# Recurrence gates of a two-layer hybrid encoder: products block by block, with inputs and gate values laid out anew by way of DRAM

## The chip, the cores and the metric

The kernel runs on one core of one Trainium2 chip. The metric is the device time of one execution in microseconds (us); lower is better. Engines are named as the profile names them: PE multiplies matrices and writes PSUM, ACT (scalar), DVE (vector) and POOL compute on SBUF and PSUM, SP issues the DMAs from its queue. All of them run their own instructions strictly in the order of the program and wait for each other by semaphores.

## What is computed

The reference runs two layers over 256 tokens of 1024 channels. Each layer normalises its input, projects it with one wide matrix, and feeds three mixers: A (gated spatial product), B (latent attention) and C (a gated linear recurrence). Each mixer's output is gated and projected, the three are merged, projected once more, normalised and added. The change is in mixer C, whose two gates are products with 16 separate blocks of 80 x 80 weights:

```python
xb = xc.reshape(B, S, LRU_BLOCKS, LRU_BW)                # 16 blocks of 80 channels
r = jax.nn.sigmoid(jnp.einsum('bshi,hij->bshj', xb, w_a).reshape(B, S, C) + b_a)
i = jax.nn.sigmoid(jnp.einsum('bshi,hij->bshj', xb, w_x).reshape(B, S, C) + b_x)
log_a = -LRU_C * r * softplus(-lam)
a = exp(log_a)
bterm = sqrt(max(1 - exp(2 * log_a), 0)) * (i * xc)
h = scan over time of  h = a * h + bterm
```

All inputs are float32. Every weight and activation is split into a high part that the PE takes at its fast rate and a low rest, and a product is the sum of three: high x high, high x low, low x high.

## The kernel before

Channels lie on the 128 partitions and tokens on the free dimension, so most products are matmuls of a 128 x 128 piece of weights with 256 tokens. Weights come in *chunks* of up to 128 x 2048 floats, 1 MB each. `load` fills one of three `raw` buffers by a DMA on SP's queue. `split` has ACT copy it to `whi` (L268) and DVE subtract to get `wlo` (L269), into one of three pairs. A step that uses up a chunk calls `done` (by way of `fin`), which frees the pair, splits the next chunk and issues a load for the chunk after that. Table `LATE` says whether a step does this ahead of or behind its own work on ACT and DVE.

The steps of a layer are run in the order that the table `ORDER` spells out. One step is mostly one chunk: 48 matmuls into one PSUM buffer of 128 x 512. These buffers are taken in turn from two rings: `bank` hands out `mm0` to `mm4`, `aux` three more. A step that takes a buffer must wait until ACT or DVE has read what the buffer held five takes earlier.

The names that matter: `u` and `za` are products of mixer A (`gate_a` takes the buffer of `u`, another for z, then ACT makes a sigmoid at L847, DVE four products at L848 to L857, and `split_act` the high and low part of `ya`, ACT first, at L452). `ga`, `gb`, `gc` are merge gates (a sigmoid on ACT, L875). `pa`, `pb`, `pc` are the projections, whose result DVE multiplies into `acc` (L897). `zb` and `zc` are the gates of mixers B and C (sigmoid on ACT at L973, DVE at L974). For mixer C there are `split` (high and low part of the input, once for each half of 640 channels), `stack` (copies that line up pieces of it), `la` and `lx` (the two gates, one step for each half, written `la` 0, `la` 1 and so on), and `r1`, `r2`, `r3` (the recurrence: in `r1` ACT loads a table and takes five exponentials, L942, and five tanh, L944; DVE multiplies, L940).

The 80-wide blocks don't fit into 128 partitions evenly. So `lru_gate` works on five tiles of 128 channels in a half. Blocks that cross a tile's border need products with pieces of two tiles. That makes 4 matmuls for an even tile and 6 for an odd one, 24 for each gate and half. It takes two buffers of the `bank` ring and one of `aux`, and ACT writes the sigmoid into the slot that `r1` reads (L932). The weights of one gate and half are loaded as 16 small pieces into a buffer that POOL has cleared (L205, L210).

Of the kernel before, what the change touches and what calls it, by code (L numbers as in the profile page):

```python
# [34 lines left out]
R_Q, R_KV, R_LG, R_LB, R_CW, R_CB, R_BA, R_BX, R_LAM, R_N = 0, 3, 5, 13, 21, 61, 71, 81, 91, 101  # L35
# [5 lines left out]

COL_EVEN, COL_ODD, COL_STACK, LRU_N = 0, GT * P, (GT + 2) * P, (GT + 5) * P


STACKS = ((0, ((1, 0, 32),)), (4, ((3, 96, 32),)), (2, ((1, 96, 32), (3, 0, 16))))
SH = 32
# [8 lines left out]
    ("attend", 1), ("xc", 4), ("conv", 3), ("v", 1), ("conv", 4), ("uq", 3), ("attend", 2), ("split", 1),  # L55
    ("v", 2), ("v", 3), ("attend", 3), ("split", 0), ("norm", 0), ("u", 0), ("stack", 0), ("attend", 4),
# [10 lines left out]


SE = {
# [25 lines left out]
def tile_trunk(ctx: ExitStack, tc, I, out):  # L95
# [72 lines left out]
    for l in range(L):  # L168
        for j in range(4):
            c0, n = ((C_CQ, QR), (C_CQ + QR, KVR + HR))[j // 2]  # L170
            kind = "slot" if l and j == 3 else None
            add((l, "c", j), Chunk(4, n, proj("w_in", l, j % 2 * 4 * P, 4, c0, n), kind=kind))
        for key, j in ORDER:
            if key in COLS:
                c = Chunk(KT, CW, win(l, COLS[key] + j * CW))
            elif key == "uq":
                c = Chunk(3, 384, proj("mla_w_uq", l, 0, 3, j * 384, 384), kind="heads")
            elif key == "ukv":
                c = Chunk(2, 1024, proj("mla_w_ukv", l, 0, 2, j * 1024, 1024))
# [14 lines left out]
    def load(c, parts=1, mid=None):  # L194
# [10 lines left out]
        G.memset(c.raw[:, :n], 0.0)  # L205

        def piece(row, col, r0, c0, nr, ncol):

            b = r0 // BW
            nc.sync.dma_start(  # L210
                c.raw[row : row + nr, col : col + ncol],
                I[name][l, g * 8 + b, r0 - b * BW : r0 - b * BW + nr, c0 - b * BW : c0 - b * BW + ncol],
            )

        for b in range(8):
            for k in range(GT):
                r0, r1 = max(b * BW, k * P), min(b * BW + BW, k * P + P)
                if r0 < r1 and k % 2 == 0:
                    piece(r0 - k * P, COL_EVEN + b * BW, r0, b * BW, r1 - r0, BW)
                elif r0 < r1:  # L220
                    c0, c1 = max(b * BW, k * P), min(b * BW + BW, k * P + P)
                    piece(r0 - k * P, COL_ODD + k // 2 * P + c0 - k * P, r0, c0, r1 - r0, c1 - c0)
        for n_, (m, runs) in enumerate(STACKS):
            for k, r, nr in runs:
                for b in range(8):
                    r0, r1 = max(b * BW, k * P + r), min(b * BW + BW, k * P + r + nr)
                    c0, c1 = max(b * BW, m * P), min(b * BW + BW, m * P + P)
                    if r0 < r1 and c0 < c1:
                        piece(r0 - k * P - r, COL_STACK + n_ * P + c0 - m * P, r0, c0, r1 - r0, c1 - c0)

    def split(c, parts=1, mid=None):
# [27 lines left out]
        if c.lru:  # L259
            act(hi[:, :n], c.raw[:, :n], AF.Copy)  # L260
            st = slice(COL_STACK, n)
            act(hi[SH : 2 * SH, st], c.raw[:SH, st], AF.Copy)
            V.tensor_tensor(lo[:, :COL_STACK], c.raw[:, :COL_STACK], f(hi[:, :COL_STACK]), ALU.subtract)
            V.tensor_tensor(hi[2 * SH : 3 * SH, st], c.raw[:SH, st], f(hi[:SH, st]), ALU.subtract)
            return
# [190 lines left out]
    with tc.manual_schedule():  # L456
# [74 lines left out]
        for l in range(L):  # L531
# [168 lines left out]

            def conv_stack(g):

                _, xh, xl = cv[g]
                xs, two = slot("xs", (GT, S), F32R), xm
                for src, dst in ((xh, xs[:, 3:5]), (xl, two)):
                    copy(SE.get("wide", "V"), dst[:64], f(src[:64, 2:5:2]))
                    copy(SE.get("wide2", "A"), dst[64:], f(src[64:, 0:3:2]))
                for n, (_, runs) in enumerate(STACKS):
                    for p, src in enumerate((xh, xl, xh)):
                        at = p * SH  # L710
                        for k, r, nr in runs:
                            copy(SE.get(("thin", n, p), "V"), xs[at : at + nr, n], f(src[r : r + nr, k]))
                cv[g] += (xs, two)
# [193 lines left out]
            def lru_gate(key, row):  # L907
                def step(g):
                    _, xh, xl, xs, two = cv[g]
# [3 lines left out]
                    for m0 in range(0, GT, 2):  # L913
                        ms = range(m0, min(m0 + 2, GT))
                        ps = bank() if len(ms) == 2 else aux()
                        for m in ms:
                            pm = ps[:, (m - m0) * S : (m - m0 + 1) * S]
                            e = slice(COL_EVEN + m * P, COL_EVEN + m * P + P)
                            if m % 2:
                                d = slice(COL_ODD + m // 2 * P, COL_ODD + m // 2 * P + P)  # L920
                                mm3(pm, wh[:, d], wl[:, d], xh[:, m], xl[:, m], True, False)
                                mm3(pm, wh[:, e], wl[:, e], xs[:, 3 + m // 2], two[:, m // 2], False, True)
                            else:
                                n = (0, 4, 2).index(m)
                                d = slice(COL_STACK + n * P, COL_STACK + n * P + P)
                                mm3(pm, wh[:, e], wl[:, e], xh[:, m], xl[:, m], True, False)
                                mm(pm, wh[: 3 * SH, d], xs[: 3 * SH, n], start=False, stop=True)
                        if ms[-1] == GT - 1:
                            fin(c, key, 0)
                        for m in ms:  # L930
                            b = row + g * GT + m
                            act(o[:, m], ps[:, (m - m0) * S : (m - m0 + 1) * S], AF.Sigmoid, bias=pt[:, b : b + 1])  # L932
# [57 lines left out]
            def rows(_):  # L990
# [8 lines left out]
                "la": lru_gate("la", R_BA), "lx": lru_gate("lx", R_BX), "r1": recur1, "r2": recur2, "r3": recur3,  # L999
# [113 lines left out]
```

## Time and profile before

| | |
|---|---|
| median of 3 runs | 798.22 us (797.47 to 798.29) |
| the profiled execution | 798.34 us, of which the span in the trace is 796.6 us |
| instructions | 15355, of them 6445 matmuls |
| busy: PE | 788.1 us, 99% of the span |
| busy: DVE, ACT, POOL | 548.9, 469.3, 70.5 us |
| moved by DMA | 137.87 MB, 173 GB/s on average |

The profile's page gives busy times by engine and the groups of instructions by line. The timeline lists single instructions of an engine: start, duration, what it is, and in brackets how long the engine stood idle before it and for whom. The windows give busy time, the clock that the PE was granted (1.00 is full speed) and the DMAs' rate in a stretch.

### The profile page before, as it was taken

What the parts mean: (1) busy time and instruction counts of PE and PEld (TensorE: products, weight loads), DVE (VectorE), ACT (ScalarE), POOL (GpSimd) and SP (SyncE); (2) the same over time, 40 slices, a digit from 0 to 9 for tenths busy, and PEclk for the clock granted to TensorE, in tenths of its full rate; (3) what the DMA queues carried; (4) which work ended last, traced back from release to release, by engine and by line L of the source; (5) the groups of instructions that cost most, each with busy time, mean ns of one, the idle gap of its engine ahead of it and who ended that gap; (6) DMA issues with size and microseconds to landing.
All of it is one profiled execution on the core that took longest, in us unless ns stands there. A gap on an engine that the chain in (4) does not pass through costs nothing.

```text
span 796.6 us, 15355 instructions
## 1 busy us (share of the span) xinstructions
PE 788.1 (99%) x6445; PEld 780.2 (98%) x6445; DVE 548.9 (69%) x712; ACT 469.3 (59%) x689; POOL 70.5 (9%) x110
## 2 busy tenths in 40 slices
PE   9999999999999999999999999999999999999996
PEld 8999999999999999999999999999999999999996
DVE  5587788666876787555666868776578578775562
ACT  5785767339855736343567776654595584544441
POOL 1100503003000000000010032031210000000000
PEclk9999999999999999999999999999999999999998
DMA  7845454344666565666357626541575656564531
GB/s 229 290 152 182 153 161 155 112 122 137 201 213 211 159 215 169 199 212 216 109 171 239 208 94 211 159 128 51 166 219 167 221 162 202 185 214 150 193 132 54
DMA packets 134205, 137.87 MB, mean 173 GB/s; under 512 B 11046, under 2 KB 130808, under 8 KB 134136
## 3 DMA queue, kind: packets, MB, share of 16 engines
q1 hardware_dynamic: 134120, 136.90, 54.3%
q8 instruction: 50, 0.82, 0.4%
q14 instruction: 19, 0.16, 0.1%
q10 hardware_dynamic: 16, 0.00, 0.0%
HBM read 135.83 MB, written 1.05 MB: 172 GB/s over the span
## 4 chain that ended last, share of the span: by engine, by line
PE 94%; DMA 2%; issue 1%; DVE 1%; ACT 1%; SPq 0%; POOL 0%; POOLq 0%; DVEq 0%; ACTq 0%
PE mm L308 25%; PE mm L307 25%; PE mm L309 25%; PE mm L431 2%; PE mm L433 2%; PE mm L432 2%; DMA raw<-in_w_in_dram 1%; PE aux L843 1%; PE mm L730 1%; PE aux L770 1%; PE mm L731 1%; DMA X<-in_x_dram 1%; PE mm L549 1%; PE aux L1021 1%; PE mm L1020 1%
## 5 line engine op out<-in xcount | busy, mean ns | idle before, releaser
L269 DVE TENSOR_TENSOR wlo<-raw,whi 128x2048 fp32r<-128x2048 f32 (+5 forms) x123 | 264.6, 2156 | 115.9 <-ACT whi L268 115.5
L307 PE MATMUL mm<-hT,whi 128*128 128x256 f32 x1088 | 307.1, 282 | 0.0
L309 PE MATMUL mm<-hT,wlo 128*128 128x256 f32 x1088 | 305.8, 281 | 0.3 <-DVE wlo L269 0.3
L308 PE MATMUL mm<-hT,whi 128*128 128x256 f32 x1088 | 305.6, 281 | 0.0
L268 ACT ACTIVATE whi<-raw 128x2048 fp32r<-128x2048 f32 (+5 forms) x123 | 221.0, 1802 | 66.6 <-PE mm L308 26.8
L309 PEld LDWEIGHTS mm<-hT,wlo 128*128 128x128 f32 x1088 | 205.0, 188 | 0.5 <-DVE wlo L269 0.5
L307 PEld LDWEIGHTS mm<-hT,whi 128*128 128x128 f32 x1088 | 205.0, 188 | 0.0
L308 PEld LDWEIGHTS mm<-hT,whi 128*128 128x128 f32 x1088 | 205.0, 188 | 0.0
L973 ACT ACTIVATE t<-mm 128x512 f32<-128x512 f32 x18 | 10.8, 598 | 52.2 <-PE mm L309 52.2
L397 POOL TENSOR_TENSOR rstd<-rstd,mhalf 128x1 f32<-128x1 f32 x8 | 4.4, 551 | 391.1 <-DVE rstd L396 391.1
L308 PE MATMUL mm<-yc,whi 128*128 128x256 f32 x128 | 36.0, 282 | 0.0
L308 PE MATMUL mm<-ya,whi 128*128 128x256 f32 x128 | 36.0, 282 | 0.0
L307 PE MATMUL mm<-ya,whi 128*128 128x256 f32 x128 | 36.0, 281 | 0.0
L307 PE MATMUL mm<-yc,whi 128*128 128x256 f32 x128 | 36.0, 281 | 0.0
L431 PE MATMUL mm<-whi,hT 128*128 128x256 f32 x128 | 36.0, 281 | 0.0
L308 PE MATMUL mm<-yb,whi 128*128 128x256 f32 x128 | 35.9, 281 | 0.0
L309 PE MATMUL mm<-ya,wlo 128*128 128x256 f32 x128 | 35.9, 280 | 0.0
L309 PE MATMUL mm<-yc,wlo 128*128 128x256 f32 x128 | 35.9, 280 | 0.0
L309 PE MATMUL mm<-yb,wlo 128*128 128x256 f32 x128 | 35.8, 280 | 0.0
L307 PE MATMUL mm<-yb,whi 128*128 128x256 f32 x128 | 35.8, 280 | 0.0
L432 PE MATMUL mm<-wlo,hT 128*128 128x256 f32 x128 | 35.8, 279 | 0.0
L433 PE MATMUL mm<-whi,hT 128*128 128x256 f32 x128 | 35.7, 279 | 0.0
(279 smaller groups left out, 1663.4 us busy)
## 6 DMA issues: line engine op xcount, KB each, us to landing
raw<-in_w_in_dram SPq DMA_DIRECT2D x76, 1024.0 KB
raw<-in_w_proj_a_dram SPq DMA_DIRECT2D x8, 1024.0 KB
raw<-in_w_proj_b_dram SPq DMA_DIRECT2D x8, 1024.0 KB
raw<-in_w_proj_c_dram SPq DMA_DIRECT2D x8, 1024.0 KB
raw<-in_w_out_dram SPq DMA_DIRECT2D x8, 1024.0 KB
raw<-in_mla_w_uq_dram SPq DMA_DIRECT2D x8, 576.0 KB
raw<-in_mla_w_ukv_dram SPq DMA_DIRECT2D x4, 1024.0 KB
raw<-in_w_in_dram SPq DMA_DIRECT2D x4, 640.0 KB
```

Source lines behind the costliest of these rows:

```text
L268: act(hi[:, w], c.raw[:, w], AF.Copy)
L269: V.tensor_tensor(lo[:, w], c.raw[:, w], f(hi[:, w]), ALU.subtract)
L307: mm(ps, lh, rh, start=start, stop=False)
L308: mm(ps, lh, rl, start=False, stop=False)
L309: mm(ps, ll, rh, start=False, stop=stop)
L431: mm(ps, lh, rh, start=k == 0, stop=False)
L432: mm(ps, lh, rl, start=False, stop=False)
L433: mm(ps, ll, rh, start=False, stop=k == KT - 1)
L549: mm(ps, ll, rh, start=False, stop=j % 2 * 4 + k == KT - 1)
L730: mm(sc[:, P : 3 * P], qn[:, P:], kn, start=True, stop=False)
L731: mm(sc[:, P : 3 * P], qp[:, P:], kr, start=False, stop=True)
L973: act(sg, ps, AF.Sigmoid)
```

## The change

Each half of 640 channels is now worked on as 8 blocks of 80 channels, with 80 partitions in use. The three products of a block are packed into two matmuls by stacking them along the contracted dimension. The first has 128 rows: 80 of high weights on high input, then 48 rows (K1) of high weights on low input. The second has 112 rows: 80 of low weights on high input, then the remaining 32 rows (K2) of high weights on low input. So a gate takes 16 matmuls, each giving 80 output rows, instead of 24. Two blocks share one PSUM buffer, so a gate takes four buffers, all from the `bank` ring, and none from `aux`. ACT makes eight sigmoids of 80 x 256 into four `tmp` buffers.

The stacked inputs need channels on other partitions. They get there by way of DRAM: `split` writes the high and low parts out (two DMAs for a half), `stack` reads them back as four tiles (eight DMAs), each gate writes its values out in blocks (four DMAs), and a new step `in` reads both gates back in 128-channel tiles (two DMAs of 128 x 5 x 256). All of these go on SP's queue, among the loads of weights. The copies of `stack` on ACT, DVE and POOL fall away, as do POOL's clearing and 13 of 16 load pieces for a gate's weights. In `split` for such a chunk, ACT copies 640 columns twice (128 and 48 partitions) and DVE subtracts 640 columns on 80 partitions.

The order is changed too. `ga` 0 stood between `za` 3 and `la` 0 and now stands behind `lx` 0. `r1` 0 stood ahead of `pa` 0, directly behind `lx` 0, and now stands behind `pa` 0, `in` 0, `stack` 1 and `ga` 1. `split` 0 is ahead of `split` 1, and `stack` 0 is later.

```diff
-    ("la", 0), ("lx", 0), ("r1", 0), ("stack", 1), ("pa", 0), ("ga", 1), ("pa", 1), ("la", 1), ("r2", 0),
+    ("la", 0), ("lx", 0), ("ga", 0), ("pa", 0), ("in", 0), ("stack", 1), ("ga", 1), ("r1", 0), ("pa", 1), ("la", 1), ("r2", 0),
...
             def conv_split(g):
-                xh, xl = slot("xh", (GT, S), F32R), slot("xl", (GT, S), F32R)
-                split_act(xh, xl, xc[g])
-                cv[g] = xc[g], xh, xl
+                cv[g] = [xc[g]]
+                for w in ("xh", "xl"):
+                    x = slot(w, (GT, S), F32R)
+                    if w == "xh":
+                        act(x, xc[g], AF.Copy)
+                    else:
+                        V.tensor_tensor(x, xc[g], f(cv[g][1]), ALU.subtract)
+                    d = dp.tile([GT * P, S], F32, tag=f"{w}{g}", name=nm(w))
+                    nc.sync.dma_start(d.rearrange("(k p) s -> p k s", p=P), f(x))
+                    cv[g] += [x, d]
             def conv_stack(g):
...
+                _, _, dh, _, dl = cv[g]
+                xs = [[slot("xs", (GB8 // 2, S), F32R) for _ in range(2)] for _ in range(2)]
+                for i in range(2):
+                    rows = slice(i * W2 // 2, (i + 1) * W2 // 2)
+                    bh, bl = (d[rows].rearrange("(b r) s -> r b s", r=BW) for d in (dh, dl))
+                    nc.sync.dma_start(f(xs[0][i][:BW]), bh)
+                    nc.sync.dma_start(f(xs[0][i][BW:]), bl[:K1])
+                    nc.sync.dma_start(f(xs[1][i][:BW]), bh)
+                    nc.sync.dma_start(f(xs[1][i][BW : BW + K2]), bl[K1:])
+                cv[g].append(xs)
...
             def lru_gate(key, row):
                 def step(g):
...
+                    for b0 in range(0, GB8, 2):
+                        ps, o = bank(), tmp()
+                        for i in range(2):
+                            b = b0 + i
+                            ws = slice(b * BW, (b + 1) * BW)
+                            x1, x2 = (x[b // 4][:, b % 4] for x in xs)
+                            pb = ps[:BW, i * S : (i + 1) * S]
+                            mm(pb, wh[:, ws], x1, start=True, stop=False)
+                            mm(pb, wl[: BW + K2, ws], x2[: BW + K2], start=False, stop=True)
+                        if b0 == GB8 - 2:
+                            fin(c, key, 0)
+                        for i in range(2):
+                            r = row + g * GB8 + b0 + i
+                            act(o[:BW, i * S : (i + 1) * S], ps[:BW, i * S : (i + 1) * S], AF.Sigmoid,
+                                bias=pt[:BW, r : r + 1])
+                        nc.sync.dma_start(rows[:, b0 : b0 + 2], v2(o[:BW], S))
+                    fin(c, key, 1)
+                    gates[key, g] = d
+                return step
+
+            def gate_in(g):
+                for key in ("la", "lx"):
                     o = slot(key, (GT, S))
...
+                    nc.sync.dma_start(o, gates[key, g].rearrange("(k p) s -> p k s", p=P))
                     gates[key, g] = o
```

Two places in layer 0 show what this does to the order on ACT and DVE; layer 1 has the same. In these rows `whi`, `wlo` and `raw` are the split and loaded weights, `t` the temporary buffers, `mm` and `aux` the PSUM buffers with their number, and each product's buffer is what it reads.

First ACT, from the sigmoid of `za` 3 to the gates of half 0. Before, with `la` from `mm3`, `mm4` and `aux1`, and `lx` from `mm0`, `mm1` and `aux2`:

```order
L847 ACTIVATE t4_77<-mm1_82 128x512
L260 ACTIVATE whi2_96<-raw2_91 128x1280
L262 ACTIVATE whi2_96<-raw2_91 32x384
L452 ACTIVATE ya_34_401<-t5_78 128x512
L268 ACTIVATE whi0_92<-raw0_89 128x2048
L875 ACTIVATE t6_79<-mm2_83 128x512
L932 ACTIVATE la_73_2013<-mm3_84,pt_13_349 128x256 x2
L932 ACTIVATE la_73_2013<-mm4_85,pt_13_349 128x256 x2
L268 ACTIVATE whi1_94<-raw1_90 128x2048
L932 ACTIVATE la_73_2013<-aux1_87,pt_13_349 128x256
L932 ACTIVATE lx_74_2046<-mm0_81,pt_13_349 128x256 x2
L932 ACTIVATE lx_74_2046<-mm1_82,pt_13_349 128x256 x2
```

After the change (L827 is the sigmoid of `za` 3, L239 a split of a chunk, L425 the high part of `ya`, L907 the sigmoids of the gates):

```order
L827 ACTIVATE t4_79<-mm1_84 128x512
L239 ACTIVATE whi2_98<-raw2_93 128x2048
L425 ACTIVATE ya_34_403<-t5_80 128x512
L907 ACTIVATE t6_81<-mm2_85,pt_13_351 80x256 x2
L907 ACTIVATE t7_82<-mm3_86,pt_13_351 80x256 x2
L907 ACTIVATE t0_75<-mm4_87,pt_13_351 80x256 x2
L239 ACTIVATE whi0_94<-raw0_91 128x2048
L907 ACTIVATE t1_76<-mm0_83,pt_13_351 80x256 x2
L907 ACTIVATE t2_77<-mm1_84,pt_13_351 80x256 x2
L907 ACTIVATE t3_78<-mm2_85,pt_13_351 80x256 x2
```

`la` 0 now reads `mm2`, `mm3`, `mm4`, `mm0`, and `lx` 0 reads `mm1` and then `mm2` again; the split of a whole chunk stands ahead of the last two sigmoids of `la` 0.

Second DVE, from `r1` 0 to the next two results of `pa`. Before:

```order
L940 TENSOR_TENSOR lx_74_2046<-lx_74_2046,xc_27_392 128x1280
L945 TENSOR_TENSOR u_76_2080<-a_75_2079 128x1280
L449 CAST xs_77_2093<-xh_66_1254 64x512 x2
L449 CAST xm_110<-xl_67_1255 64x512 x2
L263 TENSOR_TENSOR wlo0_93<-raw0_89,whi0_92 128x896
L264 TENSOR_TENSOR whi0_92<-raw0_89,whi0_92 32x384
L897 TENSOR_TENSOR acc_38_405<-t6_79,mm2_83 128x512
L269 TENSOR_TENSOR wlo1_95<-raw1_90,whi1_94 128x2048
L269 TENSOR_TENSOR wlo2_97<-raw2_91,whi2_96 128x2048
L897 TENSOR_TENSOR acc_38_405<-t7_80,mm4_85 128x512
```

After (L924 and L929 are the two products of `r1` 0, L240 the low part of a chunk, L877 the result of `pa` into `acc`):

```order
L877 TENSOR_TENSOR acc_38_407<-t6_81,mm1_84 128x512
L240 TENSOR_TENSOR wlo1_97<-raw1_92,whi1_96 128x2048
L924 TENSOR_TENSOR lx_83_2093<-lx_83_2093,xc_27_394 128x1280
L929 TENSOR_TENSOR u_89_2162<-a_88_2161 128x1280
L240 TENSOR_TENSOR wlo2_99<-raw2_93,whi2_98 128x2048
L877 TENSOR_TENSOR acc_38_407<-t7_82,mm3_86 128x512
```

`r1` 0 now stands between the result of `pa` 0 (`mm1`) and that of `pa` 1 (`mm3`), and the latter stands behind the split that `pa` 1 triggers, with `r1` ahead of both.

More of the change, by code (lines that the diff above doesn't have):

```diff
@@ L32 @@
 CWID = 4
[L35 to L46, printed above, removed]
+R_Q, R_KV, R_LG, R_LB, R_CW, R_CB, R_LAM, R_BA, R_BX, R_N = 0, 3, 5, 13, 21, 61, 71, 81, 97, 113
+GB8, K1 = 8, 48
+K2 = BW - K1
+W2 = GB8 * BW
 SLOT_W = 1296
@@ L54 @@
     ("uq", 2), ("v", 0),
-    ("attend", 1), ("xc", 4), ("conv", 3), ("v", 1), ("conv", 4), ("uq", 3), ("attend", 2), ("split", 1),
-    ("v", 2), ("v", 3), ("attend", 3), ("split", 0), ("norm", 0), ("u", 0), ("stack", 0), ("attend", 4),
[3 rows of a table removed]
+    ("attend", 1), ("xc", 4), ("conv", 3), ("v", 1), ("conv", 4), ("uq", 3), ("attend", 2), ("split", 0),
+    ("v", 2), ("v", 3), ("attend", 3), ("split", 1), ("norm", 0), ("u", 0), ("attend", 4),
[3 rows of a table added]
     ("zb", 3), ("r1", 1), ("pa", 3), ("pb", 0), ("r2", 1), ("gb", 1), ("pb", 1), ("r3", 1), ("zc", 0),
@@ L101, in tile_trunk @@
     sm = ctx.enter_context(tc.tile_pool(name="sm", bufs=2))
+    dp = ctx.enter_context(tc.tile_pool(name="dp", bufs=1, space=bass.MemoryType.DRAM))
     psm = ctx.enter_context(tc.tile_pool(name="psm", bufs=1, space=bass.MemoryType.PSUM))
@@ L180, in tile_trunk @@
             elif key in ("la", "lx"):
-                c = Chunk(LRU_N // P, P, lru=("lru_w_" + key[1], l, j))
+                c = Chunk(GB8, 2 * BW, lru=("lru_w_" + key[1], l, j))
             elif key in ("pa", "pb", "pc"):
@@ L204, in load @@
         name, l, g = c.lru
[L205 to L229, printed above, removed]
+        w = I[name][l, g * GB8 : (g + 1) * GB8].rearrange("b r c -> r b c")
+        r1, r2 = (v2(c.raw[:, i * W2 : (i + 1) * W2], BW) for i in range(2))
+        nc.sync.dma_start(r1[:BW], w)
+        nc.sync.dma_start(r1[BW:], w[:K1])
+        nc.sync.dma_start(r2[64 : BW + K2], w[64 - K2 :])
     def split(c, parts=1, mid=None):
@@ L259, in split @@
         if c.lru:
[L260 to L264, printed above, removed]
+            raw, r2 = c.raw[:, :W2], c.raw[64 : BW + K2, W2 : 2 * W2]
+            act(hi[:, :W2], raw, AF.Copy)
+            act(lo[64 : BW + K2, :W2], r2, AF.Copy)
+            V.tensor_tensor(lo[:BW, :W2], raw[:BW], f(hi[:BW, :W2]), ALU.subtract)
             return
@@ L321, in tile_trunk @@
     X = const.tile([P, NT, D], F32, name="X")
-    xm = const.tile([P, 2, S], F32R, name="xm")
     def layer_consts(l, rows):
+        G.memset(rows[64:R_N], 0.0)
         for name, r0, n in (
             ("mla_q_norm_g", R_Q, 3), ("mla_kv_norm_g", R_KV, 2), ("gm_ln_g", R_LG, 8), ("gm_ln_b", R_LB, 8),
-            ("lru_conv_b", R_CB, 10), ("lru_b_a", R_BA, 10), ("lru_b_x", R_BX, 10), ("lru_lambda", R_LAM, 10),
+            ("lru_conv_b", R_CB, 10), ("lru_lambda", R_LAM, 10),
         ):
@@ L330, in layer_consts @@
         nc.sync.dma_start(rows[R_CW : R_CW + 40], I["lru_conv_w"][l].rearrange("w (t p) -> (w t) p", p=P))
+        for name, r0 in (("lru_b_a", R_BA), ("lru_b_x", R_BX)):
+            nc.sync.dma_start(rows[r0 : r0 + NB, :BW], I[name][l].rearrange("(b p) -> b p", p=BW))
         return {"rows": rows}
@@ L696, in conv_split @@
             def conv_split(g):
-                xh, xl = slot("xh", (GT, S), F32R), slot("xl", (GT, S), F32R)
-                split_act(xh, xl, xc[g])
-                cv[g] = xc[g], xh, xl
-            def conv_stack(g):
[L703 to L713, printed above, removed]
+                cv[g] = [xc[g]]
[8 more added lines that the diff above has]
+                    cv[g] += [x, d]
+            def conv_stack(g):
+                _, _, dh, _, dl = cv[g]
[8 more added lines that the diff above has]
+                cv[g].append(xs)
             cv = {}
@@ L908, in step @@
                 def step(g):
-                    _, xh, xl, xs, two = cv[g]
+                    xs = cv[g][-1]
                     c = get(l, key, g)
                     wh, wl = (t.rearrange("p a b -> p (a b)") for t in (c.hi, c.lo))
-                    o = slot(key, (GT, S))
[L913 to L932, printed above, removed]
@@ L933, in step @@
-                    fin(c, key, 1)
+                    d = dp.tile([GT * P, S], F32, tag=f"{key}{g}", name=nm(key))
+                    rows = d.rearrange("(b r) s -> r b s", r=BW)
+                    for b0 in range(0, GB8, 2):
[14 more added lines that the diff above has]
+                        nc.sync.dma_start(rows[:, b0 : b0 + 2], v2(o[:BW], S))
@@ L934, in step @@
+                    fin(c, key, 1)
[3 more added lines that the diff above has]
+                for key in ("la", "lx"):
+                    o = slot(key, (GT, S))
+                    nc.sync.dma_start(o, gates[key, g].rearrange("(k p) s -> p k s", p=P))
                     gates[key, g] = o
-                return step
             def recur1(g):
@@ L998, in tile_trunk @@
                 "shift": gate_shift, "u": gate_u, "za": gate_a,
[L999 removed]
+                "in": gate_in, "la": lru_gate("la", R_BA), "lx": lru_gate("lx", R_BX), "r1": recur1, "r2": recur2, "r3": recur3,
                 "ga": gate("ga"), "gb": gate("gb"), "gc": gate("gc"),
```

2 lines of the change are left out of this document (removed), and 7 rows, old and new, of tables (ORDER, SE).

## The prediction, made before the changed kernel had run

> **What bounds the kernel now.** I read the page first: busy time by engine, then the groups of instructions.
>
> ```profile
> span 796.6 us, 15355 instructions
> PE 788.1 (99%) x6445; PEld 780.2 (98%) x6445; DVE 548.9 (69%) x712; ACT 469.3 (59%) x689; POOL 70.5 (9%) x110
> ...
> L309 PE MATMUL mm<-hT,wlo 128*128 128x256 f32 x1088 | 305.8, 281 | 0.3 <-DVE wlo L269 0.3
> ...
> DMA packets 134205, 137.87 MB, mean 173 GB/s; under 512 B 11046, under 2 KB 130808, under 8 KB 134136
> ```
>
> PE is busy for 99% of the span, and even the group of matmuls that reads the low weights, the last thing to become ready, has stood idle for only 0.3 us in all (third number, behind the bar). So before the change each matmul taken away shortens the run by its pace, and each new wait of PE lengthens it by its length. ACT and DVE have spare time on average, but the averages hide the stage that is changed. Next I read the windows around the gates of layer 0 (columns: length, then busy time of PE, PEld, DVE, ACT, POOL, then granted clock, DMA share, GB/s):
>
> ```profile
> 180.00:200.00 20.00, 20.00 (x171) 20.00 (x170) 13.32 (x11) 19.75 (x34) 7.54 (x7) 1.00 0.47 143
> ```
>
> Here ACT works for 19.75 us of 20. PE doesn't wait for it only because each PSUM buffer has been read by the time it is wanted again. Whether that holds is a question of order and of how many takes lie between two uses of a buffer. That is what I follow next, in the timelines.
>
> **Part 1, fewer matmuls.** The step `lx` 1 of before stands between the second and third of these rows of PE's timeline (start, duration, what; the first is the start of the step behind `za` 3, the last the kernel's last matmul):
>
> ```profile
> 173.56 0.36 PE L307 MATMUL mm<-hT,whi 128*128 128x256 f32 x1
> ...
> 233.27 0.28 PE L307 MATMUL mm<-xh,whi 128*128 128x256 f32 x1
> 236.13 0.29 PE L307 MATMUL mm<-hT,whi 128*128 128x256 f32 x1
> ...
> 789.70 0.28 PE L1021 MATMUL aux<-whs,mg 128*128 128x256 f32 x1
> ```
>
> Its 24 matmuls took 236.13 - 233.27 = 2.86 us, 0.119 us each; they overlap, so the 0.28 us of a row is not the pace. Two layers have two gates in two halves, 8 steps that go from 24 to 16: 64 matmuls x 0.119 = **7.6 us less**, 3.8 a layer. I take the 80-wide matmuls at the same pace, since they move the same 256 columns; nothing in the trace of before is as narrow, so this is an estimate. What ACT, DVE and POOL lose in copies, clearing and split work lies beside PE and is worth nothing by itself; it counts only where a chain below holds it.
>
> **Part 2, the ring in half 0 (stall A).** The two gates now take eight buffers out of a ring of five, all within 32 matmuls, 3.8 us. `la` 0 takes `mm2`, `mm3`, `mm4`, `mm0`; `lx` 0 takes `mm1`, which held the z of `za` 3, and then `mm2`, `mm3`, `mm4` again; `ga` 0 takes `mm0`. All but `mm1` must first be emptied by ACT's sigmoids of `la` 0, and ACT has work ahead of these. Its timeline (in brackets: idle time before, and for whom):
>
> ```profile
> 172.95 0.60 ACT L847 ACTIVATE t<-mm 128x512 f32<-128x512 f32 x1 [4.98 <-PE mm L309]
> ...
> 176.54 0.63 ACT L452 ACTIVATE ya<-t 128x512 fp32r<-128x512 f32 x1 [1.27 <-DVE t L857]
> ...
> 179.41 1.92 ACT L268 ACTIVATE whi<-raw 128x2048 fp32r<-128x2048 f32 x1 [2.23 <-PE mm L308]
> 181.23 0.58 ACT L875 ACTIVATE t<-mm 128x512 f32<-128x512 f32 x1
> 181.71 1.56 ACT L932 ACTIVATE la<-mm,pt 128x256 f32<-128x256 f32 x4
> 183.13 1.94 ACT L268 ACTIVATE whi<-raw 128x2048 fp32r<-128x2048 f32 x1
> ```
>
> I count from s, the start of `za` 3's sigmoid (172.95). ACT then splits a chunk (1.82 us, 179.41 to 181.23) and must wait for DVE's gate chain before it writes `ya`: 176.54, s + 3.59; free at s + 4.22. Gate sigmoids follow each other at 0.355 us (four from 181.71 to 183.13), and I keep that for the 80-row ones. So the first pair, `mm2`, is empty at s + 4.22 + 0.71 + 0.04 = s + 4.97. PE starts `la` 0 at s + 0.61 (173.56) and has done 16 + 4 matmuls by s + 2.99: it stops for 2.0 us. Then it follows ACT: six sigmoids until s + 6.35, then the split that stands in their middle (1.82), then the last two, so `mm0` is free for `ga` 0 at s + 8.92. Unhindered, PE would be there at s + 0.61 + 32 x 0.119 = s + 4.42. **Stall A is 4.5 us a layer**, in two stops of about 2 us. In the order of before `ga` 0 lay between `za` 3 and `la` 0, 5.7 us of PE's work in which ACT could get ahead; this cover is what the change takes away.
>
> **Part 3, the result of `pa` 1 (stall B).** Between `pa` 1 and `ga` 2 only `la` 1 takes buffers, four of them. So `ga` 2 takes the fifth, `mm3`, the one `pa` 1 filled just ahead. Who empties it is DVE (L877), and it now stands behind `r1` 0 and the split that `pa` 1 triggers, which stands behind ACT's part of the same split, behind ACT's part of `r1` 0. The pieces, ACT first, then DVE:
>
> ```profile
> 189.07 1.28 ACT L942 ACT_TABLE_LOAD   x1
> 190.37 2.11 ACT L942 ACTIVATE a<-la,sA 128x256 f32<-128x256 f32 x5
> 192.38 2.10 ACT L944 ACTIVATE la<-la,sT 128x256 f32<-128x256 f32 x5
> 194.49 1.60 ACT L447 ACTIVATE xs<-xl 32x256 fp32r<-32x256 f32 x4
> ```
>
> ```profile
> 204.55 2.29 DVE L269 TENSOR_TENSOR wlo<-raw,whi 128x2048 fp32r<-128x2048 f32 x1 [1.42 <-ACT whi L268]
> 206.76 0.68 DVE L897 TENSOR_TENSOR acc<-t,mm 128x512 f32<-128x512 f32 x1
> ```
>
> From the end g of `ga` 1 on PE: 0.04 to ACT, its split 1.82, the sigmoid of `ga` 1 0.48 (181.23 to 181.71), table load 1.30, exponentials 2.01, tanh 2.11 (189.07 to 190.37 to 192.38 to 194.49), split of `pa` 1 1.92, 0.04, DVE's split 2.21 (204.55 to 206.76), result 0.68: g + 12.6. PE gets to `ga` 2 after 48 + 16 matmuls, at g + 7.6. **Stall B is 5.0 us a layer.** Before, `la` 1 took only two buffers of this ring, so two more takes lay between `pa` 1 and the reuse of its buffer, and the same chain was hidden. For half 1 I find no stall: the step behind `lx` 1 takes the buffer of `zb` 0, whose readers are quick:
>
> ```profile
> 233.47 0.60 ACT L973 ACTIVATE t<-mm 128x512 f32<-128x512 f32 x1 [3.40 <-PE mm L309]
> ```
>
> ```profile
> 234.10 0.69 DVE L974 TENSOR_TENSOR t<-mm,t 128x512 f32<-128x512 f32 x1 [2.19 <-ACT t L973]
> ```
>
> It is free 234.79 - 233.47 = 1.3 us after the product and is wanted 1.9 us after it, since 16 matmuls of `lx` 1 lie between. The margin of half a microsecond is thin; if it is gone, what is late costs tenths, not microseconds.
>
> **Part 4, the way by DRAM.** A half now writes 1.31 MB (640 channels x 256 tokens x 4 bytes, twice), reads 1.97 MB of stacked tiles, and writes and reads 1.31 MB of gates each: 5.9 MB, 23.6 MB over four halves, on 137.87. All of it waits in SP's one queue, with loads of weights behind. The nearest rows for the rate, and for how soon a load starts:
>
> ```profile
> 241.00:242.00 1.00, 1.00 (x11) 1.00 (x10) 1.00 (x1) 0.06 (x1) 0.00 (x0) 1.00 1.09 387
> ```
>
> ```profile
> 242.37 0.37 SPq L200 DMA_DIRECT2D raw<-in_w_in_dram  x1
> ```
>
> A busy window moves 387 GB/s, against a mean of 173. The inputs of half 0 are written well ahead of `la` 0 and have slack. Tightest is the place behind `pa` 0, where `in` 0 (1.31 MB) and `stack` 1 (1.97 MB) wait behind two weight loads (2.1 MB): 5.4 MB, 14 us at 387 GB/s. `pa` 0 ends 5.71 us ahead of g, so all is there at about g + 8 to g + 9, and `la` 1 ends at g + 10 at the latest, ahead of g + 12.6. **I put the DMAs at nothing; stall B hides them.** Without stall B they would cost about 2.5 us a layer (10 against 7.6). They can't gain anything, since PE waited for no load before. Where SP waits for ACT's gate values to be written out, the loads queued behind it belong to chunks two or three steps on (5.71 us each), which covers it.
>
> The Trainium skill, page "DMA: Bandwidth & Descriptors", section "Anatomy of one DMA", gives every transfer a fixed cost of about 2 us, most of it the receipt of the write. Two round trips of write and read in a row would by that, as an estimate, bring 4 us more to the places above; the slack of `la` 0 would still be about enough, and behind stall B it would add 1 to 2 us a layer, which makes the sum 814 to 816. No row of before shows a round trip.
>
> **Part 5, the clock.** At the end of the kernel PE stops for good, and the windows (granted clock is the third number from the end) show what happens:
>
> ```profile
> 789.00:790.00 1.00, 0.98 (x9) 0.78 (x7) 0.00 (x0) 0.00 (x0) 0.00 (x0) 1.00 0.00 0
> 791.00:792.00 1.00, 0.00 (x0) 0.00 (x0) 0.67 (x2) 0.00 (x0) 0.38 (x1) 1.00 0.00 0
> 792.00:793.00 1.00, 0.00 (x0) 0.00 (x0) 0.96 (x3) 0.00 (x0) 0.00 (x0) 0.63 0.00 0
> 793.00:794.00 1.00, 0.00 (x0) 0.00 (x0) 0.00 (x0) 0.00 (x0) 0.00 (x0) 0.50 0.98 352
> ```
>
> The last matmul ended at 789.98. The clock was 1.00 until 792 and 0.63 in the next window, so it fell to 0.50 at about 792.3, 2.3 us after the stop. Stall B is longer than that, the two stops of stall A are just shorter. How long the clock stays low no row tells; my estimate is as long as it took to fall, which costs half of 2.3 us a time. Bounds are none and four (both stalls, both layers): 0 to 4.6 us. I take the two of stall B: **2.3 us**.
>
> The Trainium skill, page "TensorE: Matmul & The Clock Gate", Part 1, says that an idle window of about 3.4 us halves the clock and that about 3.4 us of activity brings it back. By it a fall would cost 1.7 us: two make 813.1 us, four 816.5, as an estimate. The trace agrees that the clock halves, and saw it fall sooner, after 2.3 us.
>
> **Sum** against the profiled run's own 798.34 us (its span of 796.6 and 1.7 around it; the median of the runs is 0.12 lower): 798.34 - 7.6 + 2 x (4.5 + 5.0) + 2.3 = **812.0 us**. Without clock losses it is 809.7, with the upper bound 814.3.
>
> **The rivals.** *The clock falls in every stop and stays low for a whole step.* A step of 5.71 us at half speed loses 2.86 us; four make 809.7 + 11.4 = 821.1, fewer or shorter ones 815 to 821. For it: A's stops of 2.0 us lie near the 2.3 seen. Against: that figure says just shorter. Chance 0.18.
>
> *Only one of the two stalls comes.* A alone gives 790.7 + 9.0 = 799.7, B alone 790.7 + 10.0 + 2.3 = 803.0. For it: B is a chain of ten pieces from a stage with another load on ACT; A hangs on ACT's wait for DVE (the 1.27 us idle ahead of `ya`). Against: both follow from the order of the program. Chance 0.14, 0.04 of it ending within 0.2% of before.
>
> *ACT and DVE keep up (the other side).* The place is the same two buffers, `mm0` at `ga` 0 and `mm3` at `ga` 2. If the relieved engines (no stack copies, narrower splits) run so far ahead that `ya` and `r1` 0 are done when PE arrives, all stops vanish: 798.34 - 7.6 = 790.7. It decides where the stalls of a layer sum to less than 3.8 us: below that the kernel is faster. For it: the page's ACT is busy only 59%. Against: 19.75 of 20 us in this stage, and both chains start from a PE step that has only just ended, so work done earlier can't shorten them. Chance 0.12.
>
> *The round trip is slow.* If the transfers behind `pa` 0 go at the mean of 173 GB/s, 5.4 MB take 31 us; `stack` 1 is there at g + 25.5, `la` 1 ends near g + 26.3 instead of `ga` 2 starting at g + 12.6: 13.7 us more a layer, 812.0 + 27.4 = 839 us. Against: the mean is low because loads wait for buffers, and bursts reach 387. Chance 0.06.
>
> **How the numbers follow.** My forecast has 0.50. The range from 800 to 821 holds it, the clock's rival and nearly all of the one-stall case; outside lie the two last rivals (0.18) and little more. About 0.2% is what a measurement of this kernel can tell from no change. Faster than that: 0.12; within it: 0.04, from the one-stall case; slower: 0.50 + 0.18 + 0.10 + 0.06 = 0.84.
>
> **What would show it.** Right: in the profile after, PE's matmuls fall by 64 x 1 to 6381 and its busy share drops to about 97%; the gate line's matmuls of `lx` 0 and the first matmul of `ga` 0 idle for ACT's L907, about 4.5 us a layer; the first matmul of `ga` 2 idles for DVE's L877, about 5 us a layer; the windows there show a clock under 1.00. Wrong: no idle time at one of these places (its term falls); idle time of `la` 1 for a DMA (the round trip is late); a pace of the gate matmuls off 0.119 us; a time under 800 or above 821 us.

## The result and the profile after

The changed kernel takes **827.37 us** (median of 4 runs, 825.95 to 828.60), against 798.25 us before (797.47 to 800.62): a ratio of 1.0359, with an interval of 1.0332 to 1.0386. That is 29 us slower. The forecast was 812.0, 14 us slower, and its range ended at 821. The profiled execution took 825.95 us. Its page first:

```profile
span 824.2 us, 15168 instructions
PE 795.2 (96%) x6381; PEld 783.0 (95%) x6381; DVE 533.7 (65%) x688; ACT 465.2 (56%) x689; POOL 39.0 (5%) x80
DMA packets 162285, 163.43 MB, mean 198 GB/s; under 512 B 16126, under 2 KB 158888, under 8 KB 162216
```

There are 64 matmuls fewer, as intended, and yet PE is busy for 7 us longer: some of its matmuls ran slowly. The view of waits says what PE waited for (total, times, longest):

```profile
PE mm L901 <- DMA xs<-xl: 8.7, 3, 5.0
PE mm L902 <- DMA xs<-xl: 5.2, 4, 1.9
PE mm L278 <- ACT t L907: 3.4, 2, 1.8
PE mm L901 <- ACT t L907: 3.2, 2, 1.7
```

Two places a layer. The waits for ACT are the two stops of stall A. The larger ones, 13.9 us in all, are for a DMA: `la` 1 waits for its stacked inputs. Of the wait for DVE's result of `pa` 1 (stall B) there is no row. PE's timeline in layer 0, from the first matmul of `la` 0 to the first of `ga` 2:

```profile
173.97 0.36 PE L901 MATMUL mm<-xs,whi 128*80 128x256 f32 x1
...
178.35 0.35 PE L901 MATMUL mm<-xs,whi 128*80 128x256 f32 x1 [1.50 <-ACT t L907]
...
182.32 0.58 PE L278 MATMUL mm<-hT,whi 128*128 128x256 f32 x1 [1.82 <-ACT t L907]
...
212.76 0.47 PE L901 MATMUL mm<-xs,whi 128*80 128x256 f32 x1 [4.99 <-DMA xs<-xl]
...
217.87 0.47 PE L902 MATMUL mm<-xs,wlo 112*80 112x256 f32 x1 [0.95 <-DMA xs<-xl]
...
219.42 0.41 PE L278 MATMUL mm<-hT,whi 128*128 128x256 f32 x1
```

The windows of the same stretch (granted clock, DMA share and GB/s at the end of a row) show the clock after each place, and how fast the DMAs moved:

```profile
180.00:182.00 2.00, 0.51 (x4) 0.26 (x3) 0.42 (x1) 2.00 (x3) 0.00 (x0) 0.77 0.72 183
182.00:184.00 2.00, 1.68 (x8) 1.68 (x9) 1.87 (x1) 2.00 (x7) 0.00 (x0) 0.50 0.98 300
186.00:188.00 2.00, 2.00 (x12) 2.00 (x12) 1.00 (x1) 0.97 (x1) 0.00 (x0) 0.52 1.10 260
...
198.00:206.00 8.00, 8.00 (x70) 8.00 (x70) 2.05 (x1) 3.68 (x3) 0.00 (x0) 1.00 1.06 357
206.00:212.00 6.00, 1.77 (x15) 1.56 (x14) 1.42 (x2) 4.65 (x11) 0.00 (x0) 0.98 1.12 230
...
220.00:222.00 2.00, 2.00 (x12) 2.00 (x11) 0.53 (x1) 2.00 (x3) 0.00 (x0) 0.50 1.05 363
```

A window of 2 us holds 19 matmuls at full clock and 12 when it is halved. The bill for layer 0: `ga` 0 starts 8.35 us after `la` 0, where 32 matmuls need 3.8, so stall A is 4.5 us. ACT's split behind `ga` 0 comes at 190.69 instead of 182.32 + 5.71, so the slow clock costs 2.6 us more. From the end of `pa` 1 (207.77, where 4.99 us of idle time begin) to `ga` 2 there are 11.65 us; 16 matmuls at full pace, the first overlapping the one before, need 1.75: 9.9 us lost. The clock stays low to 222, 1.1 us more. That makes 18.1 us; two layers and the 7.6 us gained make 28.6, and the profiled runs differ by 27.6. Layer 1 waits a little less.

Why the inputs come late stands in SP's timeline:

```profile
194.96 0.39 SPq L191 DMA_DIRECT2D raw<-in_w_proj_a_dram  x1
196.61 0.37 SPq L191 DMA_DIRECT2D raw<-in_w_in_dram  x1
197.07 0.53 SPq L918 DMA_DIRECT2D la<-la  x1
197.79 1.28 SPq L918 DMA_DIRECT2D lx<-lx  x1
199.13 2.21 SPq L689 DMA_DIRECT2D xs<-xh  x1
...
210.82 0.30 SPq L692 DMA_DIRECT2D xs<-xl  x1
```

The two loads, `in` 0 and `stack` 1 stand in one line. The last read of `stack` 1 is not even issued before 210.82, when the read of `lx` eight DMAs ahead of it has ended (DVE, which waits for `lx`, goes on at 210.83).

### The profile page after: what moved, and what is told of

It is laid out like the page before. It is cut to its first block, busy times and chain, and to the rows that moved or that the text cites. A ratio compares the mean times of both kernels' runs of the same rounds, so it can differ in the third digit from the quotient of the medians.

```text
span 824.2 us, 15168 instructions
## 1 busy us (share of the span) xinstructions
PE 795.2 (96%) x6381; PEld 783.0 (95%) x6381; DVE 533.7 (65%) x688; ACT 465.2 (56%) x689; POOL 39.0 (5%) x80
## 4 chain that ended last, share of the span: by engine, by line
PE 86%; DMA 6%; issue 2%; DVE 2%; ACT 2%; SPq 0%; POOLq 0%; POOL 0%; DVEq 0%; ACTq 0%
PE mm L278 22%; PE mm L279 22%; PE mm L280 22%; DMA lx<-lx 3%; PE mm L406 2%; PE mm L405 2%; PE mm L404 2%; DMA xs<-xl 2%; DMA raw<-in_w_in_dram 1%; PE mm L710 1%; PE aux L750 1%; PE mm L711 1%; DMA X<-in_x_dram 1%; PE mm L522 1%; DVE wlo L240 1%
## 5 line engine op out<-in xcount | busy, mean ns | idle before, releaser
L240 DVE TENSOR_TENSOR wlo<-raw,whi 128x2048 fp32r<-128x2048 f32 (+5 forms) x123 | 263.9, 2150 | 142.3 <-ACT whi L239 142.0
L239 ACT ACTIVATE whi<-raw 128x2048 fp32r<-128x2048 f32 (+5 forms) x123 | 220.4, 1801 | 76.8 <-PE mm L279 41.5
L278 PEld LDWEIGHTS mm<-hT,whi 128*128 128x128 f32 x1088 | 208.6, 192 | 4.0 <-ACT t L907 4.0
L280 PEld LDWEIGHTS mm<-hT,wlo 128*128 128x128 f32 x1088 | 208.2, 191 | 0.3 <-DVE wlo L240 0.3
L279 PEld LDWEIGHTS mm<-hT,whi 128*128 128x128 f32 x1088 | 208.5, 192 | 0.0
```

Source lines behind the costliest of these rows:

```text
L239: act(hi[:, w], c.raw[:, w], AF.Copy)
L240: V.tensor_tensor(lo[:, w], c.raw[:, w], f(hi[:, w]), ALU.subtract)
L278: mm(ps, lh, rh, start=start, stop=False)
L279: mm(ps, lh, rl, start=False, stop=False)
L280: mm(ps, ll, rh, start=False, stop=stop)
```

## Experiments

The theory after the result: the 64 matmuls are a real gain, and PE loses it to waits that follow from the place of steps: the ring (A), the late stacked inputs, and behind these the covered stall B. The main rival: one resource, the DMAs or ACT, is short in this stage whatever the order, and a wait removed comes back elsewhere.

**Three of eight buffers from the other ring.**

```diff
-                        ps, o = bank(), tmp()
+                        far = b0 >= 4 if key == "la" else b0 == 6
+                        ps, o = (aux if far else bank)(), tmp()
```

> Three of the eight buffers of each half's gates come from the three-buffer ring instead of the ring of five (the last two of la, the last one of lx). Theory (stall A is the ring's wait for the gate sigmoids, with the slow clock behind it; 4.5 + 2.3 us a layer): ga 0 now finds its buffer 0.5 us late at most, the clock stays up there, so 827.4 - 2 x (6.8 - 0.5) = 814.8 us; the wait of la 1 for its stacked inputs stays as it is, some 7 us a layer. Rival (ACT is simply late in this stage, whichever buffers are used): the stop moves to a later step, 825 us or more.

821.79 us (ratio 1.0296, 1.0277 to 1.0315). Stall A is gone (0.3 us left at `ga` 0) and the clock stays up there, but of the 14 us at that place only 5.6 arrive at the end: PE comes to `la` 1 earlier and waits there longer, 6.43 us instead of 4.99. (The edit adds a line, so L902 here is L901 above.)

```profile
208.25 0.47 PE L902 MATMUL mm<-xs,whi 128*80 128x256 f32 x1 [6.43 <-DMA xs<-xl]
```

**`stack` 1 earlier, and both edits.**

```diff
-    ("la", 0), ("lx", 0), ("ga", 0), ("pa", 0), ("in", 0), ("stack", 1), ("ga", 1),
+    ("la", 0), ("lx", 0), ("stack", 1), ("ga", 0), ("pa", 0), ("in", 0), ("ga", 1),
```

> Only stack 1 is moved, from behind in 0 to directly behind lx 0. Theory (the stacked inputs come late because they wait in SP's queue behind two loads and in 0): la 1 no longer waits for a DMA, and the wait that was covered shows: the first matmul of ga 2 waits for DVE's result of pa 1, 5.0 us a layer and about 1.3 us of slow clock, instead of 9.7 + 1.1: 827.4 - 9 = about 818 us. Rival (the DMAs together are the limit, wherever they are queued): another load or stack comes late by as much, 825 to 829 us.

835.43 us (1.0462, 1.0432 to 1.0491): slower, against both expectations. `la` 1 waits for nothing, but what stood behind `stack` 1 is late instead: `in` 0, on which `r1` 0 waits on ACT, with the splits and the result of `pa` 1 behind it. First PE, then ACT:

```profile
221.94 0.58 PE L278 MATMUL mm<-hT,whi 128*128 128x256 f32 x1 [12.80 <-DVE acc L877]
```

```profile
213.07 2.10 ACT L926 ACTIVATE a<-la,sA 128x256 f32<-128x256 f32 x5 [7.92 <-DMA la<-la]
```

> Both edits at once. Theory: neither gate waits for inputs, the ring wait of ga 0 is 0.5 us at most, and la 1 leaves the buffer of pa 1 alone, so that DVE's late result there is covered: 798.3 - 7.6 + 2 x 0.5 = 791.7 us, under the kernel before. If the longer chain by way of DRAM costs more than the matmuls bring even so, it ends over 798.

822.87 us (1.0314, 1.0297 to 1.0331). The expectation of 792 falls. PE waits up to 6.2 us for the high weights of a split that stands behind the same `r1` 0.

**The order alone, in the kernel before.** First both moves, then that of `r1` 0 alone:

```diff
-    ("u", 3), ("za", 3), ("ga", 0),
-    ("la", 0), ("lx", 0), ("r1", 0), ("stack", 1), ("pa", 0), ("ga", 1), ("pa", 1),
+    ("u", 3), ("za", 3),
+    ("la", 0), ("lx", 0), ("ga", 0), ("stack", 1), ("pa", 0), ("ga", 1), ("r1", 0), ("pa", 1),
```

> The kernel before with only the order of the change: ga 0 behind lx 0 and r1 0 behind ga 1 (gates of 24 matmuls, two buffers of the ring of five each, no DRAM). Theory (the order does harm only together with the gates' eight takes out of five buffers): 798.3 us, within 1.5. Rival (the order alone takes the cover away): stops at ga 0 or ga 2, 803 to 815 us.

> The kernel before with r1 0 alone moved behind ga 1. Theory (in the kernel before with the whole order, the 3 us wait for the low weights near 226 us comes from r1, r2 and r3 of half 0 standing in a row ahead of two splits on DVE): about 808 us, the same wait. Rival (ga 0's new place is what delays the splits): 798 us.

808.17 us (1.0122, 1.0104 to 1.0140) and 810.57 us (1.0153, 1.0132 to 1.0175). The order is not free: both moves cost 9.9 us and the later `r1` 0 alone 11.4, each against the kernel before in its own runs, without any DRAM. In each layer PE then waits 3.4 us for low weights, and in layer 0 the clock behind that wait is at 0.50 (226 to 228 us). PE first, then DVE, of the second kernel:

```profile
225.92 0.58 PE L309 MATMUL mm<-hT,wlo 128*128 128x256 f32 x1 [3.41 <-DVE wlo L269]
```

```profile
220.66 3.02 DVE L959 TENSOR_TENSOR_SCAN la<-a,lx 128x256 f32<-128x256 f32 x5
223.59 4.47 DVE L269 TENSOR_TENSOR wlo<-raw,whi 128x2048 fp32r<-128x2048 f32 x2
```

The scan of `r3` 0 starts 5.4 us later than before the change (215.24 there), and two splits stand behind it on DVE.

**The width of the reads, and the split inside `la`.** The first kernel reads `stack`'s tiles on 128 and 112 partitions, as many rows as before but from other places, so that its gates compute on other data:

```diff
-                    nc.sync.dma_start(f(xs[0][i][:BW]), bh)
...
+                    nc.sync.dma_start(f(xs[0][i]), dh[: 4 * P].rearrange("(b r) s -> r b s", r=P))
```

> Stack reads the same number of rows of 1 KB, but as four reads a half of 128 or 112 partitions instead of eight of 80, 48, 80 and 32, from other places of the written inputs (the gates compute on wrong data). Theory (the reads of stack move at some 230 GB/s with the DMA engines full because each covers few partitions): they go at about 360 GB/s, 1.97 MB take 5.4 instead of 8.6 us, la 1 starts about 3 us sooner: 827.4 - 2 x 3 = 821 us. Rival (reading back what was written out is slow as such): no change, 826 to 829 us.

825.78 us (1.0331, 1.0302 to 1.0359), not to be told from the change. From 208 to 212 us the rate is 239 GB/s against 234 in the changed kernel, and the last stacked input is there at 216.69 instead of 217.87. So the theory of narrow reads falls:

```profile
208.00:212.00 4.00, 0.32 (x1) 0.15 (x1) 3.00 (x3) 3.98 (x8) 0.00 (x0) 0.96 1.11 239
```

The second puts the entry `"la": 1` into the table `LATE`.

> Only the split that la triggers is moved behind la's last two sigmoids (a table entry for la). Theory: the second stop of half 0, at the first matmul of ga 0, shrinks from 1.8 us to 0.2; the first, 1.5 to 1.7 us, stays. If the clock falls for that one alone, all gained is 1.6 us a layer at that place; if it falls only because two stops come together, the 24 slow matmuls (2.3 us a layer) go too. Since la 1 waits for its transfers anyway, at most half of it reaches the end: 823 to 826 us. Rival (the stop was not made by that split): 827.4 us with a stop of 1.8 us as before.

821.74 us (1.0288, 1.0266 to 1.0311). The second stop is gone, the first stands, and the clock doesn't fall for it:

```profile
178.21 0.35 PE L901 MATMUL mm<-xs,whi 128*80 128x256 f32 x1 [1.71 <-ACT t L907]
```

```profile
182.00:184.00 2.00, 2.00 (x19) 2.00 (x18) 1.84 (x1) 2.00 (x7) 0.00 (x0) 1.00 0.93 256
```

So stall A is made as predicted. Of its two stops one alone does not halve the clock, both do, which the forecast had not counted.

**Everything apart, on SP's queue.** The edit of the ring, and `stack` 1 behind `lx` 0, `in` 0 behind `pa` 1, `la` 1 behind `ga` 2, `r1`, `r2`, `r3` of half 0 behind `pa` 2, `lx` 1 and `zb` 1.

> Three of eight buffers from the other ring, stack 1 directly behind lx 0, in 0 behind pa 1, la 1 behind ga 2, and r1, r2, r3 of half 0 apart from each other, behind pa 2, lx 1 and zb 1. Theory (all that the change costs are waits that follow from the place of steps; the 64 matmuls are a real gain of 7.6 us): each transfer has a step or two more to land, and no split stands behind the recurrence: 798.3 - 7.6 + about 1 = 792 us. Rival (the round trips' traffic in the one queue makes some load late wherever they stand): 798 us or more, with a wait for a load or a split in place of these.

822.05 us (1.0305, 1.0278 to 1.0332): the rival. A load of weights issued behind `stack` 1 (198.50) lands 9.8 us later, and ACT's split waits for it:

```profile
208.26 1.92 ACT L239 ACTIVATE whi<-raw 128x2048 fp32r<-128x2048 f32 x1 [9.88 <-DMA raw<-in_w_proj_a_dram]
```

**POOL's queue.** All round trips are issued by POOL (`nc.sync.dma_start` to `nc.gpsimd.dma_start` in `conv_split`, `conv_stack`, `lru_gate` and `gate_in`); then the ring's edit on top, then `in` 0 and `stack` 1 behind `lx` 0 and `r1` 0 behind `pa` 0. POOL has little else to do (39.0 us in the changed kernel), and it computes on SBUF alone: none of its rows names a PSUM buffer.

> All DMAs of the round trips (the inputs out and in, the gate values out and in) are issued from POOL's queue instead of SP's; nothing else is changed. Theory (they are late because they stand in SP's one queue behind loads that wait for a raw buffer to be split, and the loads behind them; the engines' rate would do): in 0 and stack 1 start as soon as the gates are written, about 189 us instead of 197 to 211, la 1 doesn't wait for a DMA, and the wait for DVE's result of pa 1 at ga 2 shows, 5 us a layer and 1.3 of slow clock: about 818 us. Rival (the transfers are limited by the 16 engines' rate of 230 GB/s): la 1 still waits 5 us or more, 824 to 829 us.

820.77 us (1.0281, 1.0255 to 1.0306). `in` 0 is issued at 188.38 instead of 197.07 and the last read of `stack` 1 at 200.79 instead of 210.82. `la` 1 waits once in layer 0 (1.9 us) and not in layer 1, and the covered stall B comes out, at the place and nearly of the size that was predicted (4.2 and 5.0 us in the two layers):

```profile
216.56 0.58 PE L278 MATMUL mm<-hT,whi 128*128 128x256 f32 x1 [4.25 <-DVE acc L877]
```

> POOL's queue, and three of eight buffers of each half from the other ring. Theory: no waits at lx 0, ga 0, la 1 or for the buffer of pa 1; what is left is the price of r1 0's new place, which the kernel before with that move alone showed, 12 us: 798.3 - 7.6 + 12 = about 803 us, with the wait for low weights behind r3 0. Rival (that price belongs to the waits already counted): 792 us.

> As the last one, and in 0 and stack 1 directly behind lx 0, and r1 0 directly behind pa 0, one step later than it stood before the change. Theory: nothing is late any more, the 64 matmuls are a real gain: 798.3 - 7.6 + about 1.5 = 792 us. Rival (r1 0 now waits on ACT for in 0, with splits behind it): 798 us or more and a wait for high weights near pa 1.

813.61 us (1.0194, 1.0172 to 1.0215) and 813.66 us (1.0194, 1.0169 to 1.0219). Stalls A and B are gone. PE comes to `la` 1 earlier and waits there again, four times in layer 0: 1.2 to 2.0 us each for inputs in the first kernel, 0.7 to 2.2 in the second, where one of the four is for a split. The slow clock follows. So the queue alone is not all.

**The reads of `stack` 1 where the DMAs are idle.** On top of the last kernel, `stack` 1 stands behind `za` 3:

> As the last one (POOL's queue, three of eight buffers from the other ring, in 0 behind lx 0, r1 0 behind pa 0), and stack 1 ahead of la 0, so that its 1.97 MB are read about 178 us, when the 16 DMA engines had nothing to do in the last run (0 GB/s from 174 to 180 us), instead of among two loads and in 0. Theory (la 1's wait is a matter of the DMA engines' time in that stage: they are full from 188 to 216 us): la 1 waits for nothing, and the matmuls' gain shows, 798.1 - 7.6 + about 2 = 792 to 795 us. Rival (the round trips cost as much wherever the reads are put): 808 us or more, with a wait for a load.

**796.71 us** (median of 10 runs; ratio 0.9975, 0.9962 to 0.9988): under the kernel before. All that is left of waits around the gates:

```profile
PE mm L280 <- DVE wlo L240: 1.4, 4, 0.6
...
PE mm L278 <- DVE acc L877: 0.9, 2, 0.5
PE mm L278 <- ACT t L908: 0.6, 2, 0.3
```

```profile
PE 784.5 (99%) x6381; PEld 774.9 (97%) x6381; DVE 533.2 (67%) x688; ACT 465.3 (59%) x689; POOL 93.5 (12%) x160
```

With the 2.9 us of these rows 793.5 us were to be expected (798.2 - 7.6 + 2.9). Most of the other 3 us is in the same eight stops, since the rows count only the time in which nothing ran. Two of them, at `ga` 0:

```profile
177.42 0.28 PE L903 MATMUL aux<-xs,wlo 112*80 112x256 f32 x1
177.99 0.39 PE L278 MATMUL mm<-hT,whi 128*128 128x256 f32 x1 [0.29 <-ACT t L908]
178.22 0.28 PE L279 MATMUL mm<-hT,whi 128*128 128x256 f32 x1
178.81 0.39 PE L280 MATMUL mm<-hT,wlo 128*128 128x256 f32 x1 [0.31 <-DVE wlo L240]
```

Matmuls that overlap start 0.12 us apart. Here 0.57 us lie between the first two starts and 0.23 between the next two, so a stop of 0.29 us costs 0.56. Counted by starts the eight stops cost 5.1 us, which makes 795.7; the last 1.0 us is less than the spread of these ten runs (794.4 to 798.9).

What still was open is whether the queue matters once the reads are early. One kernel puts this one's round trips back on SP, the other moves `stack` 1 alone, in the changed kernel:

> The last kernel with its round trips back in SP's queue; all else is kept (three of eight buffers from the other ring, stack 1 ahead of la 0, in 0 behind lx 0, r1 0 behind pa 0). Theory that the DMA engines' time in the stage decides: 797 to 799 us, no wait for a DMA at la 1. Theory that the place in SP's queue decides (a DMA that waits for its producer holds up the loads behind it): 803 us or more, with waits for splits whose load came late.

> The changed kernel with stack 1 alone moved ahead of la 0, on SP's queue. Engines' time decides: la 1 waits for nothing, in 0 has less beside it and lands by 206 us, and the wait for DVE's result of pa 1 at ga 2 shows with about 5 us and 1.3 of slow clock a layer; the two stops of half 0 stay: about 818 us. The queue decides: the loads behind stack 1 come late too, 825 us or more, with waits for high or low weights.

818.71 us (1.0231, 1.0212 to 1.0251) and 829.85 us (1.0382, 1.0367 to 1.0398). The queue alone is worth about 21 us here, each kernel taken against the kernel before in its own runs. In the first, SP's timeline shows the gate values written only behind the reads of `stack` 1, at 189.43 where POOL's queue issued them at 178.23:

```profile
180.58 0.53 SPq L689 DMA_DIRECT2D xs<-xh  x1
...
189.43 2.74 SPq L910 DMA_DIRECT2D la<-t  x3
```

```profile
206.60 2.10 ACT L927 ACTIVATE a<-la,sA 128x256 f32<-128x256 f32 x5 [5.96 <-DMA la<-la]
```

```profile
212.55 0.58 PE L278 MATMUL mm<-hT,whi 128*128 128x256 f32 x1 [7.71 <-ACT whi L239]
```

`in` 0 is late by that, `r1` 0 waits on ACT, the split behind it too, and PE for that. In the second, `in` 0 is late in the same way and `ga` 2 waits 8.4 us for DVE (11.2 in the other layer).

## Why the prediction was wrong

**Part 1 held**: 64 matmuls fewer, at the pace that was assumed. `lx` 1 of the changed kernel, from its first matmul to the first of the next step:

```profile
237.64 0.28 PE L901 MATMUL mm<-xs,whi 128*80 128x256 f32 x1
...
239.56 0.28 PE L278 MATMUL mm<-hT,whi 128*128 128x256 f32 x1
```

That is 1.92 us for 16 matmuls, 0.120 each, where 24 took 2.86 before: 0.94 us less, 7.5 in eight steps. The best kernel gives most of that back in short stops and nets 1.5.

**Stall A held to a tenth**: `mm0` was forecast free 8.92 us after the sigmoid of `za` 3; `ga` 0 started at 182.32, with that sigmoid at 173.36, 8.96 us after. The cause was right too: other buffers for three of the eight takes removed it.

**Stall B was there but covered.** In the changed kernel `la` 1 ended later still. Its 4 to 5 us came out where the inputs were in time. Its chain also runs later than forecast where `r1` 0 waits for `in` 0, a wait that the forecast's chain did not hold: in the changed kernel the result of `pa` 1 was done at 216.7, not at g + 12.6 = 214.6 (g is 202.0, where ACT's split behind `ga` 1 starts).

**Part 4 is the step that failed**: "I put the DMAs at nothing; stall B hides them." The last stacked input was there when PE went on at 217.87, g + 15.9, not g + 8 to 9. The forecast divided 5.4 MB by the 387 GB/s of one window of 1 us. From the end of `pa` 0 (g - 5.71 = 196.3) the same 5.4 MB took 21.6 us, 250 GB/s on average: 357 from 198 to 206 us, 230 from 206 to 212 with `stack`'s reads in flight, and the 16 engines busy all the time in both. The rate is one half of it and the place in the queue the other: on POOL's queue, where the same reads are issued 9 to 10 us earlier, `la` 1 waits 1.9 us in one layer and not at all in the other. The rival of the slow round trip had the right place and wait, but its price came from the mean of 173 GB/s: 31 us for the 5.4 MB, about as far off as the forecast's 14 on the other side. The sentence in the same part that the loads behind SP's waits are covered failed too: on SP's queue each place tried for `stack` 1 and `in` 0 made something else late. The section that this part cites (the Trainium skill, page "DMA: Bandwidth & Descriptors", section "Anatomy of one DMA") is written for transfers issued by POOL, while those of the change were issued by SP; no run here measures such a fixed cost by itself.

**Part 5 was mis-sized.** No slow clock was forecast for stall A, whose stops were "just shorter" than 2.3 us. They are, but they come 4 us apart and halved the clock together, for 2.6 us a layer; with one of them left it stayed up (the kernel with `la`'s split moved behind). The Trainium skill, page "TensorE: Matmul & The Clock Gate", Part 1, speaks of an idle window of about 3.4 us; the two stops sum to 3.3 and the clock did fall, so idle time in one piece of that length was not needed here.

The sum, by its terms: forecast -7.6 + 9.0 + 10.0 + 2.3 = 13.7 us. Measured, twice layer 0: -7.6 + 9.0 for A + 19.8 for the late inputs (instead of B) + 7.4 for slow clock outside these = 28.6.

The order's own price was not forecast at all: `r1` 0 moved behind `ga` 1 delays `r3` 0 and the splits behind it by 5.4 us, which cost the kernel before 11.4 us. In the changed kernel no row shows this price by itself; that it lies under the late inputs is not shown.

## What to carry to other kernels

A transfer that takes the place of copies needs its own line in the sum: its bytes over the rate that a window of several us shows with such reads in it, not over a burst, and with what stands ahead of it in its queue. Where one queue serves a steady stream of loads and round trips that wait for producers, each delays the other; here they needed a queue of their own and a stretch in which the DMAs were idle, and taking away either, with all else kept, cost 21 or 17 us. A stall removed ahead of a late transfer is largely given back at that transfer (here 8.6 of 14.2 us), so the last chain must go first. And a stop costs more than its idle row: one of 0.29 us cost 0.56 by the starts of the matmuls.

## What the runs showed of the hardware

From 206 to 212 us, with the reads of `stack` in flight, the full engines moved 230 GB/s, where loads of weights, with rows of 1 KB as well, moved at 383. More partitions a read changed it little (239 against 234). Nor do the loads beside them explain it all. In the kernel of 796.71 us these reads were alone from 176 to 178 us (the next transfers were issued at 178.23 and 178.78) and moved at 252, at a DMA share of 0.92. The changed kernel's loads first, then these reads:

```profile
176.00:178.00 2.00, 0.85 (x8) 0.60 (x5) 1.97 (x3) 1.05 (x3) 0.00 (x0) 1.00 1.08 383
176.00:178.00 2.00, 1.71 (x16) 1.47 (x13) 2.00 (x2) 1.42 (x4) 1.51 (x3) 1.00 0.92 252
```

Why they are slower was not settled: the rows of the high part are read twice, and another layout in DRAM was not tried.

The clock fell with two stops of 1.5 and 1.8 us within 4 us of each other, and came back after 5.6 us of PE's work (182.3 to 188). For a single stop of 1.7 us it didn't fall. It need not fall within a stop: in the kernel with everything apart two stops of 0.86 and 1.82 us left it at 1.00, and it fell at 214, when PE had been at work again for 1.4 us.

```profile
210.23 0.39 PE L278 MATMUL mm<-ya,whi 128*128 128x256 f32 x1 [0.86 <-ACT whi L239]
212.56 0.38 PE L280 MATMUL mm<-ya,wlo 128*128 128x256 f32 x1 [1.82 <-DVE wlo L240]
```

```profile
212.00:214.00 2.00, 1.44 (x12) 1.45 (x13) 2.00 (x3) 2.00 (x4) 0.00 (x0) 1.00 0.32 38
214.00:216.00 2.00, 2.00 (x12) 2.00 (x11) 1.34 (x1) 2.00 (x6) 0.00 (x0) 0.50 0.97 315
```
